# Moves of four tiles in place of two, and a reordered stream of loads and stores, in a scaled matmul with an added tensor

## Chip, cores, metric

One core of a Trainium2 chip. The metric is the device time of one execution in microseconds, the median of several. PE is TensorE (the matmul engine), DVE is VectorE, ACT is ScalarE, POOL is GpSimd, SP is SyncE, which here issues every transfer. Before: 210.29 us, median of 3 runs (210.13 to 210.51).

## The reference

```python
batch, m, k, n = 16, 512, 1024, 768          # all float32
x: (16, 512, 1024)   weight: (1024, 768)   scale: 0.1   add_value: (16, 512, 768)
return (scale * np.matmul(x, weight) + add_value).astype(np.float32)
```

Seen as rows there are 8192 of them, 64 tiles of 128. Every byte of x (33.6 MB), add (25.2), weight (3.1) and out (25.2) crosses once: 87.03 MB.

## The kernel before

All transfers stand in one list and are issued by SyncE in that order; each entry is a kind (x load, weight load, add load, out store), a first tile and a number of tiles. An x load needs free slots among 16, an add load needs free slots among 32, which hold the results too.

```python
STREAM = [
    ("x", 0, 3), ("w", 0, 2), ("w", 2, 2), ("x", 3, 1), ("w", 4, 4), ("a", 0, 8),
    ("x", 4, 4), ("x", 8, 8), ("a", 8, 8), ("x", 16, 8), ("a", 16, 8), ("x", 24, 8),
    ...                                        # cut
    ("o", 32, 8), ("a", 56, 8), ("o", 40, 8), ("o", 48, 8), ("o", 56, 5), ("o", 61, 3),
]
```

PE needs x transposed, in bf16. Up to tile 13, GpSimd casts a tile, PE transposes it (as pairs of bf16 in an fp32) and DVE evacuates it, which means that it copies PE's result out of PE's output memory. From tile 14 on, ScalarE and GpSimd cast and move 32-partition quadrants, and DVE turns the 32x32 blocks, so that PE is spared ("moves" and "turns" below are these two):

```python
def move_pair(t0, half):                       # cut to its core
    src = xs[:, k:k + 2, :].rearrange("p i (c b k) -> p (i c) b k", b=4, k=64)
    for b in range(4):
        for a, move in ((2 * half, nc.scalar.copy), (2 * half + 1, nc.gpsimd.tensor_copy)):
            move(moved[t0][32 * b:32 * b + 32, :, a, :], src[32 * a:32 * a + 32, :, b, :])

def step():                                    # one tile; cut
    for j in range(KJ):
        if j == KJ // 2:
            if t + 1 not in in_pair:
                transpose(t + 1)               # PE, then an evacuation on DVE
            cast_to(...)
            # the two halves of a pair's moves, five and six tiles ahead
        product(t, j, BOTH)                    # 512 and 256 columns; three product buffers
    finish(t, BOTH[0], 0, N)                   # DVE: scale * product + add, in place
    if in_pair.get(t + 4) == t + 4:
        turn_moved(t + 4)                      # DVE, 128x1024
```

## Time and profile before

| | before |
|---|---|
| time | 210.29 us |
| span from first to last instruction | 208.4 us |
| data queue, share of 16 engines' span | 97.9% |
| PE busy | 177.1 us (85%) |
| ACT, POOL, DVE busy | 129.9, 135.2, 104.1 us |
| last finish on DVE; last store lands | 200.3; 207.5 us |

The profile is of one execution. A row of digits has the busy share of 40 equal slices in tenths. A group's line has count, busy time, mean ns of one, then the idle time before it and what ended that. A line of SyncE's waits has the total, the number of waits and the longest. "Lead" below means how long before the landing of the transfer ahead of it a transfer was issued: the larger it is, the surer the queue still has work; the least in the steady part of the two kernels, 8.75 and 9.7 us, cost nothing that the landing times show. The granted clock is the share of full speed at which PE was allowed to run. The lines themselves stand in the prediction.

### The profile page before, as it was taken

The page shows a single profiled execution, that of the slowest core. Times are in us where ns is not written, and L with a number is a line of the kernel's source. Part 1 is how long each engine was busy: PE and PEld are TensorE (multiplying, and loading weights), DVE is VectorE, ACT ScalarE, POOL GpSimd, SP SyncE. Part 2 cuts the span into 40 slices and gives each one's busy share as a digit, 9 for nine tenths or more (in the row PEclk, how much of TensorE's full clock was granted, in tenths as well). Part 3 has the DMA queues.
Part 4 walks back from the last instruction along what each step waited for, and adds up shares of the span by engine and source line. Part 5 has one row for each costly group of instructions (what it writes and reads, how often), then busy time and mean ns, then how long its engine had stood idle before and what let it go on. Part 6 is the DMA issues. An engine that isn't in the chain of part 4 may idle for free.

```text
span 208.4 us, 2843 instructions
## 1 busy us (share of the span) xinstructions
PE 177.1 (85%) x1059; PEld 108.4 (52%) x1080; DVE 104.1 (50%) x113; ACT 129.9 (62%) x210; POOL 135.2 (65%) x219
## 2 busy tenths in 40 slices
PE   0498339999999999999999999999959996799930
PEld 0355125666666666666666666666626563456510
DVE  0514713555675555566666645475054651555620
ACT  2421100540299999997999559992899919996000
POOL 1310051428699999999999759993899939997000
PEclk9999958999999999999999999999999999999995
DMA  6999999999999999999999999999999999999994
GB/s 229 413 440 448 420 459 406 440 453 415 402 464 434 413 415 425 458 415 428 415 439 451 407 436 425 450 428 407 439 426 437 453 404 426 434 437 425 423 414 187
DMA packets 4461, 87.21 MB, mean 418 GB/s; under 512 B 480, under 2 KB 480, under 8 KB 1120
## 3 DMA queue, kind: packets, MB, share of 16 engines
q1 hardware_dynamic: 4448, 87.03, 97.9%
q8 instruction: 8, 0.13, 0.2%
q14 instruction: 5, 0.04, 0.0%
HBM read 61.87 MB, written 25.17 MB: 418 GB/s over the span
## 4 chain that ended last, share of the span: by engine, by line
DMA 44%; PE 38%; POOL 10%; SPq 1%; issue 1%; DVE 1%; POOLq 0%; DVEq 0%
PE mm L170 36%; DMA out_dram<-ao 17%; DMA ao<-in_add_value_dram 15%; DMA xs<-in_x_dram 12%; POOL va L110 9%; PE tp L149 2%; DVE ao L178 1%; SPq L93 1%; SPq L250 1%; POOL xb L139 1%; SPq L256 0%; POOLq L139 0%; DVEq L178 0%
## 5 line engine op out<-in xcount | busy, mean ns | idle before, releaser
L170 PE MATMUL mm<-w_bf,xt 128*128 128x512 bf16 (+1 forms) x1003 | 170.6, 327 | 8.3 <-DVE ao L178 6.0
L110 ACT CAST va<-xs 32x512 bf16<-32x512 f32 x200 | 123.2, 616 | 46.0 <-DMA xs<-in_x_dram 43.5
L170 PEld LDWEIGHTS <-xt 128*128 128x128 bf16 x1024 | 101.0, 99 | 74.8 <-issue 5.5
L110 POOL CAST va<-xs 32x512 bf16<-32x512 f32 x200 | 121.7, 608 | 20.8 <-DMA xs<-in_x_dram 11.9
L178 DVE SCALAR_TENSOR_TENSOR ao<-mm,ao 128x768 f32<-128x768 f32 (+2 forms) x62 | 57.2, 935 | 40.3 <-PE mm L170 34.0
L119 DVE STREAM_TRANSPOSE xt<-va 128x1024 f32<-128x1024 f32 x25 | 31.1, 1244 | 29.5 <-POOL va L110 29.0
L139 POOL CAST xb<-xs 128x1024 bf16<-128x1024 f32 x11 | 11.2, 1043 | 29.4 <-DMA xs<-in_x_dram 21.8
L149 PE MATMUL tp<-identity,xb 128*128 128x128 f32 x56 | 10.2, 317 | 14.5 <-DVE xb L135 7.7
L149 PEld LDWEIGHTS tp<-identity,xb 128*128 128x128 f32 x56 | 7.7, 163 | 16.4 <-issue 7.7
L157 DVE COPY xt<-tp 128x1024 bf16<-128x1024 bf16 x10 | 6.9, 688 | 10.8 <-PE tp L149 10.8
L157 ACT COPY xt<-tp 128x512 bf16<-128x512 bf16 (+1 forms) x7 | 4.1, 655 | 9.2 <-PE tp L149 9.2
L97 DVE CAST w_bf<-ao 128x768 bf16<-128x768 f32 x8 | 4.0, 555 | 4.9 <-DMA ao<-in_weight_dram 4.9
L135 DVE CAST xb<-xs 128x512 bf16<-128x512 f32 x3 | 1.9, 695 | 7.1 <-DMA xs<-in_x_dram 7.1
L137 POOL CAST xb<-xs 128x512 bf16<-128x512 f32 x2 | 1.6, 835 | 5.9 <-DMA xs<-in_x_dram 5.9
L137 ACT CAST xb<-xs 128x512 bf16<-128x512 f32 x1 | 0.6, 619 | 5.1 <-DMA xs<-in_x_dram 5.1
L237 DVE TENSOR_TENSOR ao<-ao 128x768 f32<-128x768 f32 x3 | 2.7, 953 | 1.1 <-DMA ao<-in_add_value_dram 1.1
L206 DVE TENSOR_SCALAR ao<-mm 128x768 f32<-128x768 f32 x2 | 1.8, 953 | 2.5 <-PE mm L170 2.5
L137 ACT ACT_TABLE_LOAD x1 | 1.3, 1283 | 0.7 <-PEq L281 0.7
L203 ACT ACTIVATE ao<-mm 128x768 f32<-128x768 f32 x1 | 0.8, 817 | 0.0
masks.py:197 POOL MEMSET identity<- 128x128 f32 x1 | 0.2, 205 | 0.3 <-POOLq L281 0.3
masks.py:199 POOL TENSOR_SCALAR_AFFINE_SELECT identity<-identity 128x128 f32<-128x128 f32 x1 | 0.3, 293 | 0.1
L281 POOL MEMSET const-float32-0.0<- 128x1 f32 x1 | 0.1, 98 | 0.2 <-issue 0.2
(3 smaller groups left out, 0.3 us busy)
## 6 DMA issues: line engine op xcount, KB each, us to landing
xs<-in_x_dram SPq DMA_DIRECT2D x7, 4096.0 KB, 23.9
ao<-in_add_value_dram SPq DMA_DIRECT2D x8, 3072.0 KB, 31.1
out_dram<-ao SPq DMA_DIRECT2D x7, 3072.0 KB, 31.3
xs<-in_x_dram SPq DMA_DIRECT2D x1, 2048.0 KB, 24.4
out_dram<-ao SPq DMA_DIRECT2D x1, 1920.0 KB, 9.9
xs<-in_x_dram SPq DMA_DIRECT2D x1, 1536.0 KB, 6.4
ao<-in_weight_dram SPq DMA_DIRECT2D x2, 768.0 KB, 8.5
ao<-in_weight_dram SPq DMA_DIRECT2D x1, 1536.0 KB, 13.2
```

The costliest lines, as they stand in the source:

```text
L93: nc.sync.dma_start(ao[:, s:s + n, :].rearrange("p (c r) n -> p c (r n)", r=2), w_v[:, j // 2:(j + n) // 2, :])
L97: nc.vector.tensor_copy(w_bf[:, j + i, :], ao[:, s + i, :])
L110: move(moved[t0][32 * b:32 * b + 32, :, a, :], src[32 * a:32 * a + 32, :, b, :])
L119: nc.vector.transpose(xt.rearrange("p i c m -> p (i c m)"), moved.pop(t0).bitcast(fp32).rearrange("p c a k -> p (c a k)"))
L137: other(xb[:, K // 2:K], src[:, K // 2:K])
L139: nc.gpsimd.tensor_copy(xb, src)
L149: nc.tensor.transpose(tp[:, c, :], pairs[:, c * P:(c + 1) * P], identity)
L157: evacuate(xt_tiles[t][:, c:c + q, :].bitcast(bf16), tp[:, c:c + q, :].bitcast(bf16))
L170: nc.tensor.matmul(mm_tiles[t, cols[0]][:, n0:n1], lhs(t, j), w_bf[:, j, n0:n1], start=(j == 0), stop=(j == KJ - 1))
L178: nc.vector.scalar_tensor_tensor(a, mm_tiles[t, part][:, n0:n1], float(scale), a, op0=mybir.AluOpType.mult, op1=mybir.AluOpType.add)
L237: nc.vector.tensor_add(ao[:, t, :], ao[:, EARLY_AT + t, :], ao[:, t, :])
L250: nc.sync.dma_start(xs[:, k:k + n, :], rows(x_v, s, n))
```

## The change

Its intent: fewer and longer moves on ScalarE and GpSimd (four tiles per instruction, from tile 12), PE transposes for two tiles fewer, and a stream with larger transfers at the head (four x tiles, two weight halves), x tiles 4 to 7 ahead of the first add load, and the last x group in two halves.

```diff
 STREAM = [
-    ("x", 0, 3), ("w", 0, 2), ("w", 2, 2), ("x", 3, 1), ("w", 4, 4), ("a", 0, 8),
-    ("x", 4, 4), ("x", 8, 8), ("a", 8, 8), ("x", 16, 8), ("a", 16, 8), ("x", 24, 8),
-    ("a", 24, 8), ("o", 0, 8), ("x", 32, 8), ("o", 8, 8), ("a", 32, 8), ("x", 40, 8),
...
+    ("x", 0, 4), ("w", 0, 4), ("w", 4, 4), ("x", 4, 4), ("a", 0, 8), ("x", 8, 8),
+    ("a", 8, 8), ("x", 16, 8), ("a", 16, 8), ("o", 0, 8), ("x", 24, 8), ("a", 24, 8),
+    ("x", 32, 8), ("o", 8, 8), ("a", 32, 8), ("x", 40, 8), ("a", 40, 8), ("o", 16, 8),
+    ("x", 48, 8), ("a", 48, 8), ("x", 56, 4), ("o", 24, 8), ("o", 32, 8), ("x", 60, 4),
+    ("a", 56, 8), ("o", 40, 8), ("o", 48, 8), ("o", 56, 6), ("o", 62, 2),
 ]
-MOVED = [14, 16, 18, ... 62]
+MOVED = [12, 16, 20, ... 60]
-    va_pool = ctx.enter_context(tc.tile_pool(name="va_pool", bufs=3))
+    va_pool = ctx.enter_context(tc.tile_pool(name="va_pool", bufs=2))
...
+        src = xs[:, k:k + 4, :].rearrange("p i (c b k) -> p (i c) b k", b=4, k=64)
+        for a in range(4):
+            move = nc.scalar.copy if a % 2 == 0 else nc.gpsimd.tensor_copy
+            move(moved[t0][32 * b:32 * b + 32, :, a, :], src[32 * a:32 * a + 32, :, b, :])
...
-                    for half in range(2):
-                        if in_pair.get(t + 6 - half) == t + 6 - half:
-                            move_pair(t + 6 - half, half)
+                    for b in range(4):
+                        if in_four.get(t + 8 - b) == t + 8 - b:
+                            move_four(t + 8 - b, b)
...
-            if in_pair.get(t + 4) == t + 4:
-                turn_moved(t + 4)
+            if t + 4 in in_four and t % 2 == 0:
+                turn_pair(t + 4)
```

## The prediction

> **What bounds the kernel now.** I read first the page's slices and DMA part, then the windows at both ends, then what the issuing queue (SyncE) waits for, then the compute groups.
>
> ```profile
> span 208.4 us, 2843 instructions
> ...
> PE   0498339999999999999999999999959996799930
> ...
> DMA  6999999999999999999999999999999999999994
> ...
> DMA packets 4461, 87.21 MB, mean 418 GB/s; under 512 B 480, under 2 KB 480, under 8 KB 1120
> ...
> q1 hardware_dynamic: 4448, 87.03, 97.9%
> ```
>
> The DMA row is at 9 in 38 of 40 slices, and the one data queue fills 97.9% of 16 engines' span. PE is also at 9 for most of it, so the page alone does not decide between the two. The windows do (columns: window, length, busy time and count of PE, PEld, DVE, ACT, POOL, clock, DMA share, GB/s):
>
> ```profile
> 2.00:3.00 1.00, 0.00 (x0) 0.00 (x0) 0.00 (x0) 0.01 (x1) 0.00 (x0) 1.00 0.58 172
> 3.00:28.00 25.00, 13.70 (x71) 8.52 (x72) 10.43 (x16) 5.47 (x9) 2.66 (x3) 0.97 1.02 429
> ...
> 100.00:140.00 40.00, 39.74 (x244) 24.10 (x247) 22.44 (x23) 35.08 (x58) 34.35 (x57) 1.00 1.00 431
> 140.00:180.00 40.00, 34.14 (x206) 20.38 (x209) 18.40 (x19) 30.64 (x51) 30.61 (x51) 1.00 1.00 430
> 180.00:204.00 24.00, 19.33 (x117) 11.34 (x117) 11.88 (x13) 10.77 (x18) 10.98 (x19) 1.00 0.99 424
> ```
>
> PE loses 6 us from 140 to 180 and the rate stays at 430 GB/s; PE is idle almost half of 3 to 28 and the rate is 429. The bytes flow at one rate whatever the engines do. The chain of waits gives PE 38% and GpSimd 10%, but it names who released whom, and a queue that holds several transfers hides those releases. How deep it is, the queue's own waits and the times to landing tell:
>
> ```profile
> SPq L250 <- ACT va L110: 63.7, 5, 19.5
> SPq L264 <- DVE ao L178: 41.8, 4, 22.5
> ...
> SPq L250 <- POOL va L110: 14.7, 5, 10.5
> ```
>
> ```profile
> ao<-in_add_value_dram SPq DMA_DIRECT2D x8, 3072.0 KB, 31.1
> out_dram<-ao SPq DMA_DIRECT2D x7, 3072.0 KB, 31.3
> ```
>
> SyncE waits 63.7 us in five waits for quadrant moves on ScalarE before it may issue x loads, but a 3 MB transfer that needs 3.15 MB / 430 GB/s = 7.3 us lands 31 us after its issue: some 24 us of work lie ahead of it. In the trace's landing times, 3 MB transfers follow one another by 7.25 to 7.5 us and 4 MB x transfers by 9.7 to 9.9 us (one by 10.9). The least lead in the steady part (issue before the landing of the transfer ahead) is 8.75 us, for the x load issued at 54.59. The waits are therefore free: the bound is 87.03 MB in one queue, 87.03 / 0.430 = 202.4 us.
>
> **What the Trainium skill says.** "DMA: Bandwidth & Descriptors", section Specifications, gives a fabric ceiling of 435 GB/s for the 16 engines, and an HBM share per core of about 358. The trace agrees with the first (429 to 431 in full windows) and not with the second. The same page, section Rules for kernel authors, asks for at least 1 MiB per transfer; before has three below it (512 and twice 768 KB), all at the head and queued behind each other, where 3 to 28 us still shows 429 GB/s, so merging them should buy little. "ScalarE: Activation LUTs", section What ACT_TABLE_LOAD costs, gives 186 ns + 0.833 ns per element without pointer operands: 612 ns at 512 elements, where the trace has 616. "TensorE: Matmul & The Clock Gate", section What's actually happening, has the clock halve after an idle window of about 3.4 us; the trace shows 0.58 and then 0.50 from 26 to 30 us, after PE has stood since about 23.
>
> **The change part by part.**
>
> *Moves.* Two tiles took 16 copies of 32x512, four take 16 of 32x1024.
>
> ```profile
> L110 ACT CAST va<-xs 32x512 bf16<-32x512 f32 x200 | 123.2, 616 | 46.0 <-DMA xs<-in_x_dram 43.5
> L110 POOL CAST va<-xs 32x512 bf16<-32x512 f32 x200 | 121.7, 608 | 20.8 <-DMA xs<-in_x_dram 11.9
> L119 DVE STREAM_TRANSPOSE xt<-va 128x1024 f32<-128x1024 f32 x25 | 31.1, 1244 | 29.5 <-POOL va L110 29.0
> L139 POOL CAST xb<-xs 128x1024 bf16<-128x1024 f32 x11 | 11.2, 1043 | 29.4 <-DMA xs<-in_x_dram 21.8 <-PE tp L149 4.0 <-ACT xt L157 3.5
> ```
>
> ScalarE: 186 + 0.833 x 1024 = 1039 ns (estimate from the page that fitted at 512). GpSimd: the 128x1024 cast takes 1043 ns. So each engine has 13 fours x 8 = 104 moves x 1.04 = 108 us in place of about 122: some 14 us less, for two tiles more. With 40 ns between instructions, a group of eight tiles takes 16 x 1.08 = 17.3 us, under the 24.4 us in which the queue moves an eight's x, add and out (9.8 + 7.3 + 7.3). All of it lies beside the queue: 0 on the end.
>
> *Tiles 12 and 13* leave PE's transposes: 8 of them (0.44 us per tile) and two evacuations of 0.69 us go, one turn of 1.24 us comes. PE -0.9 us, DVE about 0. Off the end.
>
> *The wait that grows.* A turn now waits for a whole four, and DVE runs in order: the turn of tile 12 stands before the evacuations of 10 and 11, yet needs eight moves per engine between which GpSimd casts tiles 8 to 11. I walk it: the landings of a never dry queue are x0 8.3, weights 12.1 and 15.9, x4 20.8, add 0 28.1, x8 37.9, add 8 45.2, x16 55.0, add 16 62.3, out 0 69.6, x24 79.4. GpSimd from 37.9: 4 casts x 1.08 + 8 x 1.08 = 13 us, to 51. DVE turns at 52.3, so PE stands from about 46 to 53, may fall to half clock, and reaches tile 12 at about 60 (before: 58.5). But x24 is issued at about 51 where the work ahead lasts to 69.6: lead 18 us.
>
> *Later leads by the same walk* (moves of a four 8.7 us after the landing or after the four before): x32 needs the fours 16 and 20, with only two move buffers, done near 73; the queue lasts to 86.7, lead about 13. x40 needs 24 and 28, near 97 against 111: 14. Add 40 needs out 8 landed (103.8), with add 32 and x40 behind it: 17. Add 48 needs out 16 (135.5), with x48 behind: 9.8, the least of the steady part. x60 about 140 against 172. Nowhere does it run dry.
>
> *The head.* 2 MB first instead of 1.5: products start 1.3 us later; x4 to x7 land at 20.8 instead of 28.1, because add 0 goes behind them. Bytes in the queue stay. Row times in the packet records: 12 KB 462 ns, 4 KB 159, 16 KB 615, 32 KB 1214. The merged first load saves (462 + 159 - 615) x 8 rows per engine = 0.05 us; tiles 56 to 63 in two halves cost (2 x 615 - 1214) x 8 = 0.13 us. One transfer less: no separate gap is seen between landings, 0. Sum +0.1 us.
>
> *The tail.* After add 56 both versions have 22 us of out transfers (7.3 + 7.3 + 7.3). Add 56 lands near 185 in both, and finishing tile 56 waits for it (before: DVE at 185.65). Three product buffers let PE be at tile 59 then; five tiles x 2.62 us + 0.4 end at 200. In before the last out is issued at 200.32 and lands at 207.46, 7.1 us for 1.2 MB (2.7 us at rate): about 2 us of that is issue and landing, 2 us still queue. After: out 56 to 61 is issued at about 195 with the queue full to 199, the last 0.8 MB at about 200 with the queue full to 204. Same end. Sum of all parts: +0.1 us on 210.29, less perhaps 0.2 of the one slow x transfer of before (10.9 where 9.8 is usual), which may fall otherwise.
>
> **The rivals.** (1) The queue runs dry where a turn or a move of four comes late, or because two move buffers serve in place of three. For it: SyncE's 63.7 us behind ScalarE's moves, and the granularity doubled. Against it: leads of 9.8 us or more. If moves took 1.5 us, or GpSimd and DVE slowed each other, leads would shrink by some 4 us per four and time could rise to 212 to 215. (2) Compute becomes the end: PE, stalled near 50 and then at half clock, is late at tile 61. For it: only about 2 us of slack at the tail, and four tiles' turns gathered behind x60, which is loaded late (landing about 177, moves to 186). Then each us beyond 2 counts: 211 to 213. (3) The lighter engines win: 14 us less on ScalarE and GpSimd. For it: they are at 9 in most slices and stand in the chain. Against: the rate does not react to them. The most it can recover is idle queue inside the stream, well under 1 us: 209.5.
>
> **Range and chances.** The path that sets the end is unchanged within 0.1 us, run spread is 0.4 us: 210.2, with 209.6 to 211.0 for 8 in 10, wider above because both live rivals point up. Faster by 2% means 206.1, which is less than the bytes at 430 GB/s plus 2.5 us of start, 3.5 of landing and the 1.9 between span and time: 1%. Slower than 214.5 needs rival 1 in full: 3%. Within: 96%.
>
> **What would show it.** Right: DMA at 9 in 38 slices and share near 98%; moves at about 1.04 us x104 on each engine; ScalarE about 115 us busy (129.9 - 123.2 + 108), GpSimd about 119 (two casts fewer); PE with a gap near 46 to 53 that the DMA row does not show; last out landing near 207.4. Wrong: a DMA slice under 9 inside the stream, moves over 1.2 us, a landing distance clearly over 7.3 or 9.9 us, or the last finish after 202.

## The result

After: 210.41 us, median of 6 runs (210.05 to 210.48); before, beside it: 210.22 us, median of 6 (210.12 to 210.51). The ratio is 1.0004 with a 95% interval of 0.9991 to 1.0017: the same. (Ratios are the mean time of one kernel's fast runs over that of the other's of the same rounds, so not quite the ratio of the medians.)

The page of after, the lines that answer to those of before:

```profile
span 208.7 us, 2639 instructions
...
PE   0389919997699999999999999999968999999940
...
DMA  6999999999999999999999999999999999999993
...
q1 hardware_dynamic: 4432, 87.03, 97.7%
```

204 instructions fewer, PE's dips in other places, and the DMA row as it was: 38 slices at 9, the same bytes, the same share. By windows of after (length, busy time and count of PE, PEld, DVE, ACT, POOL, clock, DMA share, GB/s):

```profile
3.00:28.00 25.00, 16.95 (x83) 10.13 (x84) 7.75 (x14) 5.47 (x9) 6.70 (x7) 1.00 1.01 430
28.00:60.00 32.00, 25.91 (x146) 16.37 (x150) 16.96 (x21) 12.54 (x13) 16.51 (x16) 0.89 1.00 429
...
100.00:140.00 40.00, 39.74 (x242) 24.01 (x246) 22.90 (x24) 31.57 (x31) 31.63 (x31) 1.00 1.00 430
```

PE has 3.3 us more work from 3 to 28 than before (x tiles 4 to 7 come earlier), then stands 6 us of the next 32 and runs at half clock in part of them. The rate does not notice: 430, 429, 430 GB/s. What SyncE waits for:

```profile
SPq L250 <- ACT va L110: 53.8, 5, 23.7
SPq L256 <- DMA out_dram<-ao: 53.4, 3, 26.1
SPq L264 <- DVE ao L178: 43.5, 4, 15.0
```

Ten us less behind ScalarE's moves, and 53 us behind out stores (34 before), because an add load now follows sooner upon the store that frees its slots. All are waits of an issuer that is ahead. The leads in the trace's landing times, against those walked in the prediction: 19.5 us for x24 (18 foretold), 15.3 for x32 (13), 14.2 for x40 (14), 16.9 for add 40 (17), 9.7 for add 48 (9.8, the least). The moves themselves:

```profile
L110 ACT CAST va<-xs 32x1024 bf16<-32x1024 f32 x104 | 108.4, 1043 | 54.3 <-DMA xs<-in_x_dram 53.0
L110 POOL CAST va<-xs 32x1024 bf16<-32x1024 f32 x104 | 107.6, 1034 | 36.3 <-DMA xs<-in_x_dram 31.8
L120 DVE STREAM_TRANSPOSE xt<-va 128x1024 f32<-128x1024 f32 x26 | 32.2, 1237 | 24.4 <-POOL va L110 24.4
```

1043 and 1034 ns for twice the elements of 616 and 608: ACT is now busy for 115.2 us, POOL for 119.1, 15 and 16 us less than before. The saved time shows up as longer waits for x. Last, the new wait, in PE's own order of time in after (start, length, what, count, and in brackets the idle time before it with its end):

```profile
31.28 2.74 PE L170 MATMUL mm<-w_bf,xt 128*128 128x512 bf16 x8 [4.44 <-DVE xt L157]
...
49.71 1.46 PE L170 MATMUL mm<-w_bf,xt 128*128 128x512 bf16 x7
53.82 1.79 PE L170 MATMUL mm<-w_bf,xt 128*128 128x512 bf16 x8 [2.65 <-DVE xt L157]
```

The first stand, 4.44 us, is at the head and was not foretold; the point-by-point part below comes back to it. The second, 2.65 us, is for the evacuation of tile 10, which sits in DVE's order behind the first turn, and the turn waits for GpSimd's last move until 51.94. After it the granted clock is 0.5 for 3.4 us. Tile 12 is finished at 64.9 us, against 61.5 before: PE is 3.4 us behind, and the end of the program does not move.

### The profile page after: what moved, and what is told of

It reads as the page before. It is cut to its first block, busy times and chain, and to the rows that moved or that the text cites. A ratio compares the mean times of both kernels' runs of the same rounds, so it can differ in the third digit from the quotient of the medians.

```text
span 208.7 us, 2639 instructions
## 1 busy us (share of the span) xinstructions
PE 180.2 (86%) x1051; PEld 108.8 (52%) x1072; DVE 103.0 (49%) x112; ACT 115.2 (55%) x114; POOL 119.1 (57%) x121
## 3 DMA queue, kind: packets, MB, share of 16 engines
q1 hardware_dynamic: 4432, 87.03, 97.7%
## 4 chain that ended last, share of the span: by engine, by line
DMA 46%; POOL 25%; PE 21%; issue 2%; SPq 1%; DVE 1%; POOLq 0%
DMA xs<-in_x_dram 46%; POOL va L110 23%; PE mm L170 21%; POOL xb L139 2%; DVE ao L178 1%; SPq L250 0%; SPq L93 0%; SPq L256 0%; POOLq L110 0%; POOLq L139 0%; DVE xt L120 0%
## 5 line engine op out<-in xcount | busy, mean ns | idle before, releaser
L170 PE MATMUL mm<-w_bf,xt 128*128 128x512 bf16 (+1 forms) x1003 | 174.1, 333 | 11.6 <-DVE xt L157 7.1
L110 ACT CAST va<-xs 32x1024 bf16<-32x1024 f32 x104 | 108.4, 1043 | 54.3 <-DMA xs<-in_x_dram 53.0
L110 POOL CAST va<-xs 32x1024 bf16<-32x1024 f32 x104 | 107.6, 1034 | 36.3 <-DMA xs<-in_x_dram 31.8
L178 DVE SCALAR_TENSOR_TENSOR ao<-mm,ao 128x768 f32<-128x768 f32 (+2 forms) x62 | 57.6, 935 | 46.0 <-PE mm L170 41.0
L120 DVE STREAM_TRANSPOSE xt<-va 128x1024 f32<-128x1024 f32 x26 | 32.2, 1237 | 24.4 <-POOL va L110 24.4
L139 POOL CAST xb<-xs 128x1024 bf16<-128x1024 f32 x9 | 9.2, 1040 | 24.1 <-DMA xs<-in_x_dram 21.8
L149 PE MATMUL tp<-identity,xb 128*128 128x128 f32 x48 | 9.2, 332 | 9.0 <-DVE xb L135 8.7
L157 DVE COPY xt<-tp 128x1024 bf16<-128x1024 bf16 x8 | 5.5, 686 | 7.6 <-PE tp L149 7.6
```

The costliest lines, as they stand in the source:

```text
L120: nc.vector.transpose(xt.rearrange("p i c m -> p (i c m)"), va.rearrange("p c a k -> p (c a k)"))
L139: nc.gpsimd.tensor_copy(xb, src)
L149: nc.tensor.transpose(tp[:, c, :], pairs[:, c * P:(c + 1) * P], identity)
L157: evacuate(xt_tiles[t][:, c:c + q, :].bitcast(bf16), tp[:, c:c + q, :].bitcast(bf16))
L170: nc.tensor.matmul(mm_tiles[t, cols[0]][:, n0:n1], lhs(t, j), w_bf[:, j, n0:n1], start=(j == 0), stop=(j == KJ - 1))
L178: nc.vector.scalar_tensor_tensor(a, mm_tiles[t, part][:, n0:n1], float(scale), a, op0=mybir.AluOpType.mult, op1=mybir.AluOpType.add)
```

## Experiments

The theory: one queue of 87.03 MB at 430 GB/s sets the time, and everything the change did lies beside it. Rivals: the two parts cancel; the moves are (or nearly are) the bound; PE, right behind the queue, sets the end.

### One part alone: fours with the old stream, pairs with the new

```diff
 # e1: after, with
-STREAM of after
+STREAM of before
 # e2: before, with
-STREAM of before
+STREAM of after
```

> One part alone: the moves of four tiles with the old order of 30 transfers. Theory (one queue that never runs dry, 87.03 MB at 430 GB/s): the same bytes, so the time of before within 0.3%, 209.8 to 210.9. Rival (the lighter moves gain and the new order gives it back): below 209.5. Rival (the coarser moves cost and the new order covers it): above 211.

> The other part alone: the moves of pairs with the new order of 29 transfers. Theory: 209.8 to 210.9. If the two parts cancel each other, this one and the one before it must lie on opposite sides of 210.2 by like amounts.

Measured in the same rounds: 210.30 us (ratio to before 0.9997, 0.9985 to 1.0009) and 210.44 us (0.9998, 0.9986 to 1.0011). Nothing cancels; each part is worth nothing by itself. But the parts do move PE. Times of the trace, last finish on DVE and last landing:

| kernel | last finish, us | last store issued | it lands | issue to landing |
|---|---|---|---|---|
| before | 200.3 | 200.3 | 207.5 | 7.1 |
| after | 201.3 | 201.3 | 207.7 | 6.4 |
| pairs, new stream (e2) | 202.1 | 202.2 | 207.5 | 5.3 |
| fours, old stream (e1) | 203.3 | 203.4 | 207.5 | 4.2 |

The compute end wanders over 3 us and the landing stays within 0.2: the last store waits in a full queue for whatever time is over. In e1 that reserve is nearly used up (before with half of its adds, below, shows 4.15 us for a store of this size into an empty queue).

### How much slower may the moves be? A quarter and a half more of them

```diff
         for a in range(4):
             move = nc.scalar.copy if a % 2 == 0 else nc.gpsimd.tensor_copy
-            move(moved[t0][...], src[...])
+            for again in range(2 if b == 0 else 1):        # e4: b < 2
+                move(moved[t0][...], src[...])
```

> After, with a quarter more moves: those of the first of the four steps are made twice, so 130 per engine in place of 104, at the 1.04 us plus 0.04 us of after: 10.8 us per four tiles, 21.6 us per eight, still under the 24.4 us in which the queue brings an eight. Theory: hidden but for the last four, whose moves start when its x lands near 178 and end about 2 us later; 210.4 to 211.5, ScalarE and GpSimd about 27 us busier each. Rival (the moves set the time): 26 x 1.08 = 28 us more on the path, up to 238.

> After, with half more moves: 156 per engine, 12 x 1.08 = 13 us per four, 25.9 us per eight, more than the queue's 24.4. Theory: now the moves are the bound: they run without a pause from x8's landing near 38.7, with 4 us of casts between: 38.7 + 4 + 13 x 13 = 212, then some 12 us of products for the last four and 5 of the last store: 226 to 233, and the queue shows slices under 9. If it stays below 214, the leads in the queue are larger than I read them; if the former run was at 238 already, the moves were the bound all along.

A quarter more: 210.74 us (ratio 1.0014, 1.0001 to 1.0027), right result. Half more: 233.71 us (1.1102). The first is hidden but for 0.3 us, and 27 us of added work per engine went nowhere; the second costs 23 us. The page of the half-more kernel:

```profile
ACT  2422003984999999999999999999999999980000
POOL 1404203999999999999999999999999999995000
...
DMA  7999999999999999999999999999999993075056
...
L111 POOL CAST va<-xs 32x1024 bf16<-32x1024 f32 x156 | 161.7, 1036 | 8.1
```

Here GpSimd has no gap from the eighth slice on and ScalarE from the eleventh, and the DMA row runs dry near the end. This is what a move-bound profile looks like, and before and after do not look like it. The point where it turns lies between 21.6 us of moves per eight tiles (hidden) and 25.9 (not), a bracket around the queue's 24.4 us of the walk. My sum of 226 to 233 for the second was 0.7 us short at its upper end.

### More bytes, fewer bytes

A store of 3.15 MB more, behind the first out store, to rows that are written properly at the end:

```diff
-... ("o", 0, 8), ("x", 24, 8) ...
+... ("o", 0, 8), ("d", 0, 8), ("x", 24, 8) ...
+        elif op == "d":
+            nc.sync.dma_start(rows(out_v, 56, n), ao[:, s:s + n, :])
```

> After with one more store of 3.15 MB behind the first out transfer, to rows that the end of the program writes again (right result). Nothing waits for it but the reload of its source. Theory (bytes in one queue): 3.15 / 0.430 = 7.3 us more, 217.2 to 218.2. Rival (PE and its waits set the time, the queue only follows): within 2 us of after.

Measured: 217.70 us (217.42 to 218.00), before in the same rounds 210.28: 7.4 us for 3.15 MB, with no work on any other engine. The right result.

```profile
DMA packets 4587, 90.34 MB, mean 418 GB/s; under 512 B 480, under 2 KB 480, under 8 KB 1120
...
q1 hardware_dynamic: 4576, 90.18, 98.0%
```

The mean rate is the 418 GB/s of before to the digit; only the bytes rose. This is the sharpest evidence for the bound.

Taking the same amount away is not its mirror image, and tells what stands behind the queue. The load of the last eight add tiles is left out (wrong in those rows), in after and in before:

```diff
-    ("a", 56, 8), ("o", 40, 8), ...
+    ("o", 40, 8), ...
```

> After without the load of the last eight add tiles (wrong on purpose in those rows): 3.15 MB fewer, 7.3 us of queue. Pure queue theory: 7.3 us less, about 203.1. My theory after reading both traces adds PE right behind: in after PE runs without a pause from 157.5 to the end near 201, the last finish does not move, and the last stores (issued near 196.6 and 201.3) find an emptier queue: last landing near 206.5, time 208.8 to 209.6. Rival (the finish of tile 56 waits for its add and delays PE): PE's end moves forward by 2 us or more and the time falls below 208.

> The same cut in before. There PE does stand for the last add (3 us near 184 to 187), so its end comes forward from 200 to about 197, and the last store of 1.2 MB needs 5.6 us from issue to landing: last landing about 202.6, time 204.8 to 206. Pure queue theory: 203. If it falls by only 1 us like after, my reading of PE's stall is wrong.

Measured: after 208.49 us (ratio to the full before 0.9900), before 207.05 (0.9853), where 3.15 MB are 7.3 us of queue. So only 2 and 3.5 us come back. In after my reading held in kind (the last finish, at 201.8, does not move), but the last store takes 4.1 us from issue to landing, with only the store before it still under way, not the 5 that I had reckoned, so the time is 0.3 us under what I expected. In before my reading was wrong: I took PE to lose 3 us to the wait for the last add, and expected its end near 197; it is at 199.9, and the time is 1 us over the range. PE's 3.0 us stall there is at 178, behind moves for x loaded late; the add had cost it 0.4 us at 186.7, for the product buffers covered the rest. PE in the full before:

```profile
178.28 7.99 PE L170 MATMUL mm<-w_bf,xt 128*128 128x512 bf16 x47 [3.05 <-DVE ao L178]
186.67 13.16 PE L170 MATMUL mm<-w_bf,xt 128*128 128x512 bf16 x78 [0.39 <-DVE ao L178]
```

Four add loads fewer (tiles 32 to 63, 12.6 MB, wrong there) take the queue out of the way in the second half (from 60 to 100 us it is still full):

```diff
-("a", 32, 8), ... ("a", 40, 8), ... ("a", 48, 8), ... ("a", 56, 8),
```

> Before without the add loads of tiles 32 to 63 (wrong on purpose there): 12.6 MB fewer, queue floor 29 us lower, near 181. So PE must set the time: its stalls of about 6 us after 150 go, end near 194.5, then 5.6 us of last store: 201 to 204. If the time reached 185, PE would not be behind the queue at all.

> After without the same loads: PE's end moves forward only by its stall of 2.6 us near 155, to about 198.7, and the last store takes 5: 205 to 207. So with the queue out of the way after would be slower than before by some 3 to 4 us, for its PE stands 4.4 and 2.7 us early on and then runs at half clock. Rival (lighter moves make the engines faster where the queue does not bind): after under before here.

Before: 200.68 us (ratio 0.9542). After: 203.52 us, its mean over the three fast runs 203.46 (0.9666); one of its four runs, the profiled one, was slow (207.5 at a lower clock) and is not used. Both are somewhat under what I expected, by 0.3 and 1.5 us, in part because the last store needs only 4.1. In before:

```profile
100.00:140.00 40.00, 40.00 (x249) 24.09 (x247) 23.80 (x24) 39.15 (x65) 37.22 (x62) 1.00 0.96 394
140.00:180.00 40.00, 40.00 (x249) 24.09 (x247) 23.88 (x24) 37.30 (x61) 37.19 (x63) 1.00 0.82 331
```

PE is busy without a gap while the DMA share falls to 0.82: this is what a PE-bound stretch looks like. So the queue's floor for these bytes (29 us less, near 181) is out of reach, PE stops the fall at 200. And with the queue out of the way there, after is the slower of the two, by 1.4%: 15 us less work on ScalarE and GpSimd is no gain even there, because these engines are not the bound there either.

### Larger transfers: what is one transfer worth?

```diff
-every transfer of eight tiles                # 29 transfers
+two of four                                  # 50 transfers
```

> After with every transfer of eight tiles cut into two of four: 50 transfers in place of 29, same bytes, rows of 16 KB and 12 KB in place of 32 and 24. Row times from the packet records (615, 462, 1214, 912 ns): 6 x loads cost (2 x 615 - 1214) x 8 = 0.13 us each, 15 add and out transfers (2 x 462 - 912) x 8 = 0.1 us each: 2.2 us in all if nothing is spent between transfers, 212 to 213.2. If each transfer had a cost of its own in the queue (0.2 us and more), 21 more of them would show as over 214.

Measured: 211.62 us (ratio 1.0066, 1.0051 to 1.0081), right result: +1.3 us, less than the 2.2 I had added up from row times.

```profile
DMA packets 7468, 87.20 MB, mean 416 GB/s; under 512 B 800, under 2 KB 800, under 8 KB 1440
...
q1 hardware_dynamic: 7456, 87.04, 98.2%
```

My row times came from few rows of before. With the medians of this run (12 KB 460 ns, 16 KB 612) and of after (24 KB 912, 32 KB 1213) the sum is 15 x 8 x 8 ns + 6 x 8 x 11 ns = 1.5 us, so the rows account for all of it. In any case 21 transfers more cost 0.06 us each at most, and one fewer, as in the change, could not be seen.

### Where PE stands

The first fours from tile 16 on, tiles 12 to 15 through PE:

```diff
-MOVED = [12, 16, ...
+MOVED = [16, ...
```

> After with the fours from tile 16 on, so tiles 12 to 15 go through PE: the 2.7 us in which PE stands near 51 to 54 and the half clock behind it go, 16 transposes of 0.11 us and four evacuations come. Theory (PE's stall is off the path): 210.0 to 210.6, the same; PE's gap near 51 gone in the trace. Rival (that stall was paid for at the end and cancelled a gain): below 209.5.

Measured: 210.79 us (ratio 1.0025, 1.0009 to 1.0040), right result; 0.2 us over my range. And the trace contradicts me on PE: the stall is not gone, it moved to the new first four and grew. DVE in order of time:

```profile
61.28 0.96 DVE L178 SCALAR_TENSOR_TENSOR ao<-mm,ao 128x768 f32<-128x768 f32 x1 [0.61 <-PE mm L170]
68.00 1.25 DVE L120 STREAM_TRANSPOSE xt<-va 128x1024 f32<-128x1024 f32 x1 [5.76 <-POOL va L110]
```

In both places where the fours were begun, the first turn waits for the x load plus eight moves with casts between, and the evacuations that PE needs stand behind it. The last finish came at 203.5, the last store was issued at 203.55 and landed at 207.68, 4.1 us later: all of the reserve is used up. But it lands when after's last store does (207.67), and this traced run took 210.49 us where that of after took 210.48. The other three runs took 210.77 to 211.04; a PE that comes still later there would explain the 0.25%, but no trace of them was kept, so its cause stays open.

To see whether the order on DVE explains why after is the slower where PE is the bound, I put each turn one step later, in the kernel with half of the adds:

```diff
-            if t + 4 in in_four and t % 2 == 0:
-                turn_pair(t + 4)
+            if t + 3 in in_four and t % 2 == 1:
+                turn_pair(t + 3)
```

> After without the add loads of tiles 32 to 63 (wrong on purpose there), as in the earlier run that took 203.5 us in its fast runs, and each turn of a pair put one step later in VectorE's order, so that the turn of tile 12 stands behind the evacuation of tile 10 and the finish of tile 9. Theory: the 2.65 us in which PE stands near 51 to 54 and the half clock of about 3.5 us behind it (1.7 us of work) go: 199.0 to 201.0, at or below the 200.7 of before with the same cut. Rival (the order of the loads at the head costs after its place): above 202.5.

Measured: 202.86 us, median of 6 (202.63 to 204.65), ratio to the full before 0.9672, where the same cut without it had 0.9666. (One of the eleven runs of before in these rounds took 280.92 us; it is left out of the ratio.) It failed: over my range of 199 to 201, no gain. The mechanism that I wanted to remove is removed, tile 12 is finished at 61.2 us as in before with the same cut, and tile 20 at 82.0 in both. Then PE waits elsewhere. What PE waited for, and DVE at that place:

```profile
PE mm L170 <- DVE xt L157: 6.8, 1, 6.8
PE mm L170 <- DVE xt L120: 2.5, 1, 2.5
```

```profile
83.67 0.96 DVE L178 SCALAR_TENSOR_TENSOR ao<-mm,ao 128x768 f32<-128x768 f32 x1 [1.64 <-PE mm L170]
90.09 1.25 DVE L120 STREAM_TRANSPOSE xt<-va 128x1024 f32<-128x1024 f32 x1 [5.45 <-POOL va L110]
```

The new wait of 2.5 us is for the turn of tile 24. Its x landed at 81.3 in this kernel and at 72.9 in before with the same cut, because the new stream puts the first out store ahead of it (7.3 of the 8.4 us), and its four then needs 8.7 us of moves. So I read it that the old stall had hidden this one: PE came late enough to find tile 24 ready (in the trace of after it runs without a pause from 56.3 to 154.9). Removing the first wait uncovered the second, of the same size. From 53.6 us on PE has no other pause, and it ends at 195.6 us where that of before with the same cut ends at 192.8, so this wait is about the whole of its lag. By the trace, then, the rival that I had named, the order of the loads, is the better part of the answer; no run with the old order tests it (the 6.8 us wait near 28 is at the head, where before has a 6.4 us one of its own).

## Why the prediction was right, point by point

- **The bound, by the rate that does not react.** Right. The extra store measured it directly (7.4 us for 3.15 MB), and each part alone, a quarter more moves, and PE 3 us later or earlier all left the time within 0.3%.
- **The moves: 104 per engine at 1.04 us, 108 us in place of 122, off the path.** Right: 1043 and 1034 ns, 108.4 and 107.6 us. That they stay hidden up to 24.4 us per eight tiles is bracketed by 21.6 (hidden) and 25.9 (23 us slower).
- **The wait that grows.** The mechanism was right, DVE's order behind the first turn, which ran at 51.94 to 53.19. The size of PE's stand was wrong: foretold from about 46, measured from 51.2 to 53.8. PE came to tile 10 some 5 us later than in the walk, and an earlier stall that the prediction had not foretold at all is about that large: 4.4 us up to 31.3, for an evacuation behind three additions that wait for the first add load, and half clock for the 3.1 us after it. The half clock after the foretold stall came as foretold, and tile 12 was finished 3.4 us later than before. (The 58.5 us that the prediction gives for tile 12 in before was misread: PE was then in the middle of it, and had ended tile 11 at about 57.4.)
- **PE 0.9 us less busy.** Wrong, 180.2 against 177.1 us. Eight transposes did go, but more products ran at half clock, in three stretches of 3.4 us where before had one of 6.8, half of which PE stood. That is about 3 us more of PE time, less the 0.9; the rest of the 3.1 is not traced. Off the path.
- **The leads.** Right within 2.3 us, the least, 9.7 us, within 0.1.
- **The head, +0.1 us.** Not to be told from zero: the last landing is 0.2 us later, and runs differ by 0.4.
- **The slow x transfer of before may fall otherwise.** It did not: 10.9 us in both. After has one late landing that before has not, add 16 after 8.3 us where 7.3 is usual. It is 0.7 us behind before when that add has landed (64.1 against 63.3 us) and 0.2 at the end, so that the close agreement with the sum of +0.1 us owes something to luck.
- **The tail: same end, about 2 us of slack.** Right. After's last store lands 6.4 us after its issue; that of the fours from tile 16 was issued 2.3 us later and landed at the same time. In before the slack was 3.0 us and not 2: its last store took 7.1 us where one of the same size took 4.15 in an empty queue. What I had not put as sharply: PE stands only these 2 to 3 us behind the queue, so lighter helpers alone gain nothing, and fewer bytes alone gain little: 3.15 MB fewer brought 1.0 and 1.5%, and 12.6 MB fewer, 14% of the bytes, 3.3 and 4.6%.

## What to carry to other kernels

When one queue is full from end to end, read the rate in windows where the engines behave differently; if it stays the same, judge any change by its bytes and by the lead with which transfers are issued, and count what it takes off the engines as nothing as long as they keep up with the queue. Know the second bound before you work on the first: a cut of 7.3 us of queue brought back 2 to 3.5. And an in-order engine that has one long wait placed early delays what stands behind it, but taking that wait out may only uncover the next.

## What the Trainium skill lacked or had wrong

- "DMA: Bandwidth & Descriptors", Bandwidth, has the HBM share of about 358 GB/s bind for transfers between HBM and SBUF. With this core alone the full windows show 429 to 432 GB/s, with 25.2 of the 87 MB being stores; of the page's figures the 435 of the fabric comes nearest. ("HBM Reference", Specifications, gives about 425 for a core alone, which is nearer than 358.)
- "DMA: Bandwidth & Descriptors", Anatomy of one DMA and Specifications, gives about 2.0 us fixed per transfer for the software path, and for transfers that SyncE issues only a time to the first byte (about 0.6). Here 21 more in a full queue cost 1.3 us in all (0.06 each); a single store of 1.2 MB into an empty queue (before with half of its adds) took 4.15 us from issue to landing, of which its bytes at 430 GB/s are 2.7.
- "TensorE: Matmul & The Clock Gate", What's actually happening, puts the fall to half clock after an idle window of about 3.4 us. Here a gap of 2.65 us was followed by 3.4 us at 0.5, about 1 us after PE had started again, and gaps of 2.55 us (the turn moved later) and 3.05 us (before, up to 178.3) by none, so the length of the gap alone does not decide.
- "GPSIMD Engine Reference", Elementwise — side-by-side cycle accounting, has per-element costs but no fixed cost for a one-input copy: 608 ns at 32x512 and 1034 at 32x1024 give 0.83 ns per element and 182 ns fixed, as on ScalarE (616 and 1043).
- "Runtime: NRT & Kernel Launch", Instruction fetch mechanics, has instructions fetched in 16 KiB blocks over a DMA queue and calls the cost mostly hidden; no page that I found says what it takes from a full data queue. In both traces a 16 KB packet of an instruction queue takes 1.06 to 1.07 us at 35.8 and 35.5 us, where a 16 KB data row takes 0.61; the x load under way then lands after 10.9 us in place of 9.7. But each trace has eight such packets, and of the others only that at 57.6 us in after goes with a landing that is late by as much (add 16), so that the one causes the other is not shown.
